# Head sums and segment sums with a 0/1 operand, as two one-pass products of the split other operand

## The chip, the cores and the metric

The kernel runs on one core of one Trainium2 chip, as one launch. The metric is device time in microseconds (us) of that launch; the median of three runs of the kernel before is 2382.67 us (2381.77 to 2384.16). The engines named below are PE (TensorE, matrix products), DVE (VectorE), ACT (ScalarE), POOL (GpSimd) and SP (SyncE, which issues the weight loads). Each engine works through its own queue in order; engines wait for one another by semaphores.

## The reference, cut to what matters

Two layers on 256 frames of width 2048, all in float32. Layer 0 has a parallel mixer (16 heads of RWKV-7 and 16 heads of Mamba-2 SSD, both of width 64), layer 1 chunked attention; each layer ends with a SwiGLU feed-forward. The change touches three sums of the mixer:

```
# RWKV-7: the norm of each head's key, and the bonus of each head
kk = heads(k * k_k)
kk = kk * lax.rsqrt(jnp.maximum(jnp.sum(kk * kk, axis=-1, keepdims=True), 1e-24))
...
bonus = jnp.sum(heads(r) * heads(k) * r_k, axis=-1, keepdims=True) * heads(v)
# SSD: decay between frames s and l of a chunk
A_cs = jnp.cumsum(Ac, axis=-1)
seg = A_cs[..., :, None] - A_cs[..., None, :]
L = jnp.where(causal, jnp.exp(jnp.where(causal, seg, 0.0)), 0.0)
```

The two sums run over the 64 channels of a head; seg[l, s] is the sum of A*dt over the frames after s up to l.

## The kernel before

All weights are streamed once from memory, in units of 256 rows by 512 columns (`stream`, lines 223 to 243). Each half of a unit is split into a high part in the one-pass float32r type (`hi`, a cast on ACT, line 240) and the remainder (`lo`, a subtraction on DVE, line 241). `mm_chunk` (lines 245 to 264) makes 512 output columns of all 256 frames: for each of 16 slices of the input, for each half of the frames, three products hi*hi, lo*hi, hi*lo (lines 260 to 262), so 96 products of 128x128 by 128x512 a chunk. The hi and lo tiles rotate through a few buffers, so the splits run only a few slices ahead of PE.

The mixer (`mixer0`, line 393) takes chunks 0 to 11 of the input projection `w_in`, called w_in#0 to w_in#11 here. Chunk 0 gives the low-rank inputs and dt; chunks 1 to 3 and 4 to 6 are the keys, receptances and values of the two halves of the RWKV heads (`rwkv_half`, line 481, called with hf = 0 and 1); 7 to 9 are the inputs of the SSD convolution (`conv_chunk`, line 771) and 10 and 11 its gate z (line 857). Then come the four chunks of the output projection `w_oab` and the rest of the network.

A half of RWKV goes through these steps. The squares kk of the keys (ACT, line 534) are summed over each head by a product with `blk`, a 128x128 matrix with ones where two channels share a head (ss, line 537), and turned into an inverse root by a logarithm and an exponential on ACT (lines 539, 540). DVE builds the tiles ar and bkv from it (lines 542 to 561). PE makes the blocks AA (line 576), DVE solves a triangular system by a row-by-row elimination in the tile NB (lines 590 to 595: 60 short instructions a half) and transposes the result three times into Sf and TG (lines 624, 625). The product ga (line 633) needs TG; from it runs a serial chain of small products over four chunks of 64 frames (gb, cx, cu, ch, cy; lines 637 to 719). The bonus is summed by a second product with `blk` (bo, line 603) and multiplied with the values on DVE (bv, line 604).

For SSD, POOL multiplies `gt` (ones where row > column) with the 8 heads' A*dt, which gives the tile L of 128 x 8 x 128 (line 826). Each head's slice is the stationary operand of a product with `tri` (ones where row <= column), four heads to a PSUM tile (sg, line 831); ACT takes the exponential (line 832), DVE multiplies it with the scores (line 833), and PE makes y (yd, line 838). There are two groups g and two halves t of the frames.

All products named so far in this part are float32 by float32, which the PE does in several passes: the trace shows two records for each.

The order on each queue is set by a list scheduler at build time, from priorities (streams of weights high) and its own table of costs; it also hands out buffers from pools. The pool `R` (tag r4) has nine buffers of 4 KB a partition: kk, ar, NB, TG, bv, bkt, uv, y and sq all live there.

```
kk[:, q, :] = square(k * k_k)                      # 534, ACT
pe.matmul(ps, lhsT=blk, rhs=kk[:, 2 * q2:2 * q2 + 2, :], start=True, stop=True)       # 537
act.activation(kk, kk, AF.Ln)                      # 539, after DVE's max with 1e-24
pe.matmul(ps[:, h, :], lhsT=L[:, 4 * h4 + h, :], rhs=tri, start=True, stop=True)      # 831
```

Of the kernel before, what the change touches and what calls it, by code (L numbers as in the profile page):

```python
# [13 lines left out]
ALU = mybir.AluOpType  # L14
# [128 lines left out]
def encoder_body(ctx: ExitStack, tc: tile.TileContext, A):  # L143
# [60 lines left out]
    def col(name, i=0, rows=P):  # L204
        return pf[:rows, _PF[name] + i:_PF[name] + i + 1]
# [187 lines left out]
    def mixer0(xt):  # L393
# [5 lines left out]
        with ExitStack() as mx:  # L399
# [5 lines left out]
            def r4(name, dt=F32, shape=(P, 4, T)):  # L405
                return R.tile(list(shape), dt, tag="r4", name=name)
# [71 lines left out]

            yst = []

            def rwkv_half(hf):
                f0 = 4 * hf
                w2 = R1.tile([96, 2, 512], F32, tag="wg", name=f"w2_{hf}")
# [6 lines left out]
                for which in range(3):  # L490
# [20 lines left out]
                    if which == 0:  # L511
# [20 lines left out]
                        kk = r4(f"kk{hf}")  # L532
                        for q in range(4):
                            act.activation(kk[:, q, :], k[:, q, :], AF.Square, scale=col("k_k", f0 + q))
                        for q2 in range(2):
                            ps = pra.tile([P, 2, T], F32, tag="ra", name=f"ss{hf}{q2}")
                            pe.matmul(ps, lhsT=blk, rhs=kk[:, 2 * q2:2 * q2 + 2, :], start=True, stop=True)
                            dve.tensor_scalar(kk[:, 2 * q2:2 * q2 + 2, :], ps, 1e-24, None, op0=ALU.max)
                        act.activation(kk, kk, AF.Ln)
                        act.activation(kk, kk, AF.Exp, scale=-0.5)  # L540
# [21 lines left out]
                    elif which == 1:  # L562
# [3 lines left out]
                        for q in range(4):  # L566
                            dve.scalar_tensor_tensor(r[:, q, :], r[:, q, :], col("r_k", f0 + q), a[:, q, :],
                                                     op0=ALU.mult, op1=ALU.mult)

                        AA = R1.tile([P, 32, 128], F32, tag="AA", name=f"AA{hf}")  # L570
                        for ch in range(4):
# [28 lines left out]
                bv = r4(f"bv{hf}")  # L600
                for q2 in range(2):
                    ps = pra.tile([P, 2, T], F32, tag="ra", name=f"bo{hf}{q2}")
                    pe.matmul(ps, lhsT=blk, rhs=r[:, 2 * q2:2 * q2 + 2, :], start=True, stop=True)
                    dve.tensor_tensor(c64(bv[:, 2 * q2:2 * q2 + 2, :]), c64(ps), bkv[:, 8 * q2:8 * q2 + 8, 128:192],
                                      op=ALU.mult)

# [189 lines left out]
            for g in range(2):  # L796
                for t in range(2):
# [2 lines left out]
            dve.tensor_tensor(SM.rearrange("p g t l -> p (g t) l"), ps.rearrange("p g t l -> p (g t) l"),  # L800
                              tri[:, None, :].broadcast_to([P, 4, 128]), op=ALU.mult)

            def hb(ap):
                return ap.rearrange("p (h v) -> p h v", v=64)

# [4 lines left out]
            for g in range(2):  # L810
# [12 lines left out]
                for t in range(2):  # L823
                    dve.tensor_tensor(hb(xc[:, t, :]), hb(xs[:, t, :]), hbc(dt[:, t, h8]), op=ALU.mult)
                    L = m4(f"L{g}{t}", (P, 8, 128))
                    pool.tensor_tensor(L, gt[:, None, :].broadcast_to([P, 8, 128]),
                                       adt[:, t, h8, None].broadcast_to([P, 8, 128]), op=ALU.mult)
                    for h4 in range(2):
                        ps = psa.tile([P, 4, 128], F32, tag="sa", name=f"sg{g}{t}{h4}")
                        for h in range(4):  # L830
                            pe.matmul(ps[:, h, :], lhsT=L[:, 4 * h4 + h, :], rhs=tri, start=True, stop=True)
                        act.activation(L[:, 4 * h4:4 * h4 + 4, :], ps, AF.Exp)
                    dve.tensor_tensor(L, L, SM[:, g, t, None, :].broadcast_to([P, 8, 128]), op=ALU.mult)
                    dve.tensor_tensor(hb(yg[:, t, :]), hb(xs[:, t, :]), hbc(rows[:, R_D + 8 * g:R_D + 8 * g + 8]),
                                      op=ALU.mult)
                    ps = psa.tile([P, 512], F32, tag="sa", name=f"yd{g}{t}")
                    for h in range(8):
                        pe.matmul(ps[:, 64 * h:64 * h + 64], lhsT=L[:, h, :], rhs=xc[:, t, 64 * h:64 * h + 64],
                                  start=True, stop=True)
                    dve.tensor_tensor(yg[:, t, :], yg[:, t, :], ps, op=ALU.add)  # L840
                    if t == 0:
                        xd = M.tile([P, 512], F32, tag="xd", name=f"xd{g}", bufs=1)
                        dve.tensor_tensor(hb(xd), hb(xc[:, 0, :]), hbc(dec[:, 0, h8]), op=ALU.mult)
                        ps = psa.tile([P, 512], F32, tag="sa", name=f"hs{g}")
                        pe.matmul(ps, lhsT=btm[:, g, :], rhs=xd, start=True, stop=True)
                        Hs = R2.tile([P, 512], F32, tag="H", name=f"Hs{g}")
                        act.copy(Hs, ps)
                    else:
                        ps = psa.tile([P, 512], F32, tag="sa", name=f"yo{g}")
                        pe.matmul(ps, lhsT=bc[:, 2 + g, P:T], rhs=Hs, start=True, stop=True)  # L850
                        yo = M.tile([P, 512], F32, tag="xd", name=f"yo{g}", bufs=1)
                        dve.tensor_tensor(hb(yo), hb(ps), hbc(dec[:, 1, h8]), op=ALU.mult)
                        dve.tensor_tensor(yg[:, t, :], yg[:, t, :], yo, op=ALU.add)
# [142 lines left out]
```

## Time and profile before

| what | value |
|---|---|
| median of three runs | 2382.67 us |
| the profiled execution's own time | 2384.66 us |
| its span in the trace | 2382.8 us (1.9 us less than its time) |
| mixer, up to the last transposes yb of the SSD output | about the first 451 us |
| PE busy in the span | 2352.1 us, 99% |
| DVE, ACT, POOL busy | 1428.8, 1267.5, 32.4 us |
| mean granted PE clock | 0.992 |

The busy time of PE is modelled from pipelined records: a product's record lasts longer than its share of the engine, so records overlap, and a busy share of 99% does not mean that no time is lost. Where a stage has waits, they are seen in the idle time before a group, in the distance between the starts of products, and in the granted clock (PEclk).

### The profile page before, as it was taken

The numbers are of one execution on the slowest core, as the hardware profiler recorded it, in microseconds if no ns is written. First come the engines' busy times: TensorE is split into PE (matmuls) and PEld (weight loads), VectorE is DVE, ScalarE is ACT, GpSimd is POOL, SyncE is SP. The second block draws the span as 40 slices with busy tenths as digits, with TensorE's granted clock in tenths as the row PEclk, the third lists the DMA queues.
The fourth block names the chain that finished last, engine by engine and source line by source line (L and its number), as shares of the span: only waits on it lengthen the run. The fifth ranks groups of instructions, "written<-read, shape, count | busy, mean of one in ns | idle before, by whom it ended". The sixth has DMA issues, their size and how long they took to land.

```text
span 2382.8 us, 31654 instructions
## 1 busy us (share of the span) xinstructions
PE 2352.1 (99%) x11426; PEld 1923.9 (81%) x11426; DVE 1428.8 (60%) x2380; ACT 1267.5 (53%) x2254; POOL 32.4 (1%) x61
## 2 busy tenths in 40 slices
PE   9999999999999999999999999999999999999998
PEld 7767777878888888888887888887888888888887
DVE  6876977765555555555557555557555555555554
ACT  6646545665545545544446555556555545454443
POOL 0000000000000000000000000000000000000000
PEclk9989999999999999999999999999999999999999
DMA  7434434666666666666665655565666666666664
GB/s 239 144 116 123 133 106 151 188 176 197 190 187 193 188 190 189 193 186 202 197 206 182 186 178 165 170 194 180 192 188 192 189 188 189 193 187 194 201 197 146
DMA packets 119357, 429.17 MB, mean 180 GB/s; under 512 B 13408, under 2 KB 13664, under 8 KB 119200
## 3 DMA queue, kind: packets, MB, share of 16 engines
q1 hardware_dynamic: 115280, 415.35, 57.2%
q0 software_dynamic: 2400, 9.18, 1.4%
q10 hardware_dynamic: 1520, 2.63, 0.4%
q8 instruction: 89, 1.46, 0.3%
q14 instruction: 68, 0.56, 0.1%
HBM read 425.01 MB, written 2.10 MB: 179 GB/s over the span
## 4 chain that ended last, share of the span: by engine, by line
PE 93%; DVE 4%; ACT 1%; DMA 1%; issue 1%; SPq 0%; DVEq 0%; ACTq 0%
PE mm_w_gu L260 13%; PE mm_w_gu L262 13%; PE mm_w_gu L261 13%; PE mm_w_dn L260 7%; PE mm_w_dn L262 7%; PE mm_w_dn L261 7%; PE mm_w_qkv L261 4%; PE mm_w_qkv L260 4%; PE mm_w_qkv L262 4%; PE mm_w_in L262 3%; PE mm_w_in L261 3%; PE mm_w_in L260 3%; PE mm_w_oab L260 1%; PE mm_w_oab L262 1%; PE mm_w_oc L262 1%; PE mm_w_oc L260 1%
## 5 line engine op out<-in xcount | busy, mean ns | idle before, releaser
L241 DVE TENSOR_TENSOR lo_w_gu<-raw_w_gu,hi_w_gu 128x512 fp32r<-128x512 f32 x704 | 485.8, 691 | 417.4 <-ACT hi_w_gu L240 414.9
L240 ACT CAST hi_w_gu<-raw_w_gu 128x512 fp32r<-128x512 f32 x704 | 438.4, 624 | 452.7 <-DVE lo_w_gu L241 404.9
L261 PE MATMUL mm_w_gu<-lo_w_gu,sh_f 128*128 128x512 f32 x1408 | 550.0, 391 | 0.0
L260 PE MATMUL mm_w_gu<-hi_w_gu,sh_f 128*128 128x512 f32 x1408 | 549.3, 390 | 0.6 <-ACT sh_f L299 0.5
L262 PE MATMUL mm_w_gu<-hi_w_gu,sl_f 128*128 128x512 f32 x1408 | 548.6, 390 | 0.0
L241 DVE TENSOR_TENSOR lo_w_dn<-raw_w_dn,hi_w_dn 128x512 fp32r<-128x512 f32 x352 | 242.8, 691 | 221.6 <-ACT hi_w_dn L240 221.0
L240 ACT CAST hi_w_dn<-raw_w_dn 128x512 fp32r<-128x512 f32 x352 | 219.0, 624 | 248.3 <-DVE lo_w_dn L241 238.6
L260 PEld LDWEIGHTS mm_w_gu<-hi_w_gu,sh_f 128*128 128x128 f32 x1408 | 264.3, 188 | 57.9 <-ACT sh_f L299 3.4
L262 PEld LDWEIGHTS mm_w_gu<-hi_w_gu,sl_f 128*128 128x128 f32 x1408 | 264.4, 188 | 55.5 <-DVE sl_f L300 1.2
L261 PEld LDWEIGHTS mm_w_gu<-lo_w_gu,sh_f 128*128 128x128 f32 x1408 | 264.4, 188 | 54.1 <-DVE lo_w_gu L241 0.3
L261 PE MATMUL mm_w_dn<-lo_w_dn,hh 128*128 128x512 f32 x704 | 274.1, 389 | 0.0
L262 PE MATMUL mm_w_dn<-hi_w_dn,hl 128*128 128x512 f32 x704 | 274.0, 389 | 0.0
L260 PE MATMUL mm_w_dn<-hi_w_dn,hh 128*128 128x512 f32 x704 | 273.9, 389 | 0.0
L241 DVE TENSOR_TENSOR lo_w_qkv<-raw_w_qkv,hi_w_qkv 128x512 fp32r<-128x512 f32 x192 | 132.2, 690 | 104.5 <-ACT hi_w_qkv L240 104.0
L240 ACT CAST hi_w_qkv<-raw_w_qkv 128x512 fp32r<-128x512 f32 x192 | 119.0, 621 | 110.3 <-DVE lo_w_qkv L241 64.8
L260 PE MATMUL mm_w_in<-hi_w_in,sh_in 128*128 128x512 f32 (+1 forms) x384 | 156.7, 408 | 1.7 <-ACT hi_w_in L240 1.7
L262 PE MATMUL mm_w_in<-hi_w_in,sl_in 128*128 128x512 f32 (+1 forms) x384 | 157.7, 411 | 0.0
L261 PE MATMUL mm_w_in<-lo_w_in,sh_in 128*128 128x512 f32 (+1 forms) x384 | 155.7, 405 | 0.0
L240 ACT CAST hi_w_in<-raw_w_in 128x512 fp32r<-128x512 f32 x184 | 112.3, 619 | 81.5 <-PE mm_w_in L262 71.5
L262 PEld LDWEIGHTS mm_w_dn<-hi_w_dn,hl 128*128 128x128 f32 x704 | 132.2, 188 | 27.6
L260 PEld LDWEIGHTS mm_w_dn<-hi_w_dn,hh 128*128 128x128 f32 x704 | 132.2, 188 | 27.3
L261 PEld LDWEIGHTS mm_w_dn<-lo_w_dn,hh 128*128 128x128 f32 x704 | 132.2, 188 | 27.2
(349 smaller groups left out, 2824.9 us busy)
## 6 DMA issues: line engine op xcount, KB each, us to landing
raw_w_gu<-in_w_gu SPq DMA_DIRECT2D x352, 512.0 KB, 3.6
raw_w_dn<-in_w_dn SPq DMA_DIRECT2D x176, 512.0 KB, 3.7
raw_w_qkv<-in_w_qkv SPq DMA_DIRECT2D x96, 512.0 KB, 3.6
raw_w_in<-in_w_in SPq DMA_DIRECT2D x92, 512.0 KB, 3.7
raw_w_oab<-in_w_oab SPq DMA_DIRECT2D x32, 512.0 KB, 4.2
raw_w_oc<-in_w_oc SPq DMA_DIRECT2D x32, 512.0 KB, 4.2
bias<-in_bias POOLq DMA_DIRECT2D x4, 768.0 KB, 6.6
x_in<-in_x SPq DMA_DIRECT2D x4, 512.0 KB, 9.0
```

The costliest lines, as they stand in the source:

```text
L240: act.copy(hi, raw[:, h, :])
L241: dve.tensor_tensor(lo, raw[:, h, :], hi.bitcast(F32), op=ALU.subtract)
L260: pe.matmul(o, lhsT=xh, rhs=h_[:, :width], start=k_ == 0, stop=False)
L261: pe.matmul(o, lhsT=xh, rhs=l_[:, :width], start=False, stop=False)
L262: pe.matmul(o, lhsT=xl, rhs=h_[:, :width], start=False, stop=k_ == nk - 1)
```

## The change

Each of the three products is replaced by two products whose 0/1 operand is stationary and is held in float32r (`blkr`, `gtr`, copied once by ACT), and whose moving operand is split into a high part (cast on ACT) and a remainder. `ones_mm` sums the two in PSUM. For the head sums the remainder is a subtraction on POOL of 128x512, two a tile (kl from kk, rl from r). For the segment sums A*dt itself is split once (adh, adl), POOL multiplies `tri` with both parts (Lr and Ll, twice the POOL products of before), and one product covers four heads, where four products stood.

```
@@ -478,6 +478,16 @@
 
             yst = []
 
+            blkr = R1.tile([P, P], F32R, tag="blkr", name="blkr")
+            act.copy(blkr, blk)
+            gtr = R1.tile([P, P], F32R, tag="gtr", name="gtr")
+            act.copy(gtr, gt)
+
+            def ones_mm(ps, ones, hi, lo):
+
+                pe.matmul(ps, lhsT=ones, rhs=hi, start=True, stop=False)
+                pe.matmul(ps, lhsT=ones, rhs=lo, start=False, stop=True)
+
             def rwkv_half(hf):
                 f0 = 4 * hf
                 w2 = R1.tile([96, 2, 512], F32, tag="wg", name=f"w2_{hf}")
@@ -532,9 +542,14 @@
                         kk = r4(f"kk{hf}")
                         for q in range(4):
                             act.activation(kk[:, q, :], k[:, q, :], AF.Square, scale=col("k_k", f0 + q))
+                        kh = r4(f"kh{hf}", F32R)
+                        kl = r4(f"kl{hf}", F32R)
                         for q2 in range(2):
+                            q4 = slice(2 * q2, 2 * q2 + 2)
+                            act.copy(kh[:, q4, :], kk[:, q4, :])
+                            pool.tensor_tensor(kl[:, q4, :], kk[:, q4, :], kh.bitcast(F32)[:, q4, :], op=ALU.subtract)
                             ps = pra.tile([P, 2, T], F32, tag="ra", name=f"ss{hf}{q2}")
-                            pe.matmul(ps, lhsT=blk, rhs=kk[:, 2 * q2:2 * q2 + 2, :], start=True, stop=True)
+                            ones_mm(ps, blkr, kh[:, q4, :], kl[:, q4, :])
                             dve.tensor_scalar(kk[:, 2 * q2:2 * q2 + 2, :], ps, 1e-24, None, op0=ALU.max)
                         act.activation(kk, kk, AF.Ln)
                         act.activation(kk, kk, AF.Exp, scale=-0.5)
@@ -566,6 +581,12 @@
                         for q in range(4):
                             dve.scalar_tensor_tensor(r[:, q, :], r[:, q, :], col("r_k", f0 + q), a[:, q, :],
                                                      op0=ALU.mult, op1=ALU.mult)
+                        rh = r4(f"rh{hf}", F32R)
+                        rl = r4(f"rl{hf}", F32R)
+                        for q2 in range(2):
+                            q4 = slice(2 * q2, 2 * q2 + 2)
+                            act.copy(rh[:, q4, :], r[:, q4, :])
+                            pool.tensor_tensor(rl[:, q4, :], r[:, q4, :], rh.bitcast(F32)[:, q4, :], op=ALU.subtract)
 
                         AA = R1.tile([P, 32, 128], F32, tag="AA", name=f"AA{hf}")
                         for ch in range(4):
@@ -600,7 +621,7 @@
                 bv = r4(f"bv{hf}")
                 for q2 in range(2):
                     ps = pra.tile([P, 2, T], F32, tag="ra", name=f"bo{hf}{q2}")
-                    pe.matmul(ps, lhsT=blk, rhs=r[:, 2 * q2:2 * q2 + 2, :], start=True, stop=True)
+                    ones_mm(ps, blkr, rh[:, 2 * q2:2 * q2 + 2, :], rl[:, 2 * q2:2 * q2 + 2, :])
                     dve.tensor_tensor(c64(bv[:, 2 * q2:2 * q2 + 2, :]), c64(ps), bkv[:, 8 * q2:8 * q2 + 8, 128:192],
                                       op=ALU.mult)
 
@@ -800,6 +821,11 @@
             dve.tensor_tensor(SM.rearrange("p g t l -> p (g t) l"), ps.rearrange("p g t l -> p (g t) l"),
                               tri[:, None, :].broadcast_to([P, 4, 128]), op=ALU.mult)
 
+            adh = M.tile([P, 2, 16], F32R, tag="adh", name="adh", bufs=1)
+            act.copy(adh, adt)
+            adl = M.tile([P, 2, 16], F32R, tag="adl", name="adl", bufs=1)
+            dve.tensor_tensor(adl, adt, adh.bitcast(F32), op=ALU.subtract)
+
             def hb(ap):
                 return ap.rearrange("p (h v) -> p h v", v=64)
 
@@ -823,12 +849,14 @@
                 for t in range(2):
                     dve.tensor_tensor(hb(xc[:, t, :]), hb(xs[:, t, :]), hbc(dt[:, t, h8]), op=ALU.mult)
                     L = m4(f"L{g}{t}", (P, 8, 128))
-                    pool.tensor_tensor(L, gt[:, None, :].broadcast_to([P, 8, 128]),
-                                       adt[:, t, h8, None].broadcast_to([P, 8, 128]), op=ALU.mult)
+                    Lr = r4(f"Lr{g}{t}", F32R, (P, 8, 128))
+                    Ll = r4(f"Ll{g}{t}", F32R, (P, 8, 128))
+                    for dst, ad in ((Lr, adh), (Ll, adl)):
+                        pool.tensor_tensor(dst, tri[:, None, :].broadcast_to([P, 8, 128]),
+                                           ad.bitcast(F32)[:, t, h8, None].broadcast_to([P, 8, 128]), op=ALU.mult)
                     for h4 in range(2):
                         ps = psa.tile([P, 4, 128], F32, tag="sa", name=f"sg{g}{t}{h4}")
-                        for h in range(4):
-                            pe.matmul(ps[:, h, :], lhsT=L[:, 4 * h4 + h, :], rhs=tri, start=True, stop=True)
+                        ones_mm(ps, gtr, Lr[:, 4 * h4:4 * h4 + 4, :], Ll[:, 4 * h4:4 * h4 + 4, :])
                         act.activation(L[:, 4 * h4:4 * h4 + 4, :], ps, AF.Exp)
                     dve.tensor_tensor(L, L, SM[:, g, t, None, :].broadcast_to([P, 8, 128]), op=ALU.mult)
                     dve.tensor_tensor(hb(yg[:, t, :]), hb(xs[:, t, :]), hbc(rows[:, R_D + 8 * g:R_D + 8 * g + 8]),
```

kh, kl, rh, rl, Lr and Ll are six new kinds of tile in the nine buffers of pool R. In the changed kernel's build the products Lr of group 0 get their buffers only behind the third chunk of the second half's serial chain, and the products sg and yd of group 0, which stood inside that chain, stand behind it.

The table of costs and the new tiles move instructions on all engines; the order of the weight loads on SP is the same. Three places follow.

First, ACT in half 0, between the squares kk and their logarithm (the second kk row behind the table load). hi_w_in are casts of streamed weights, lw, ar and c exponentials, kh the new casts. Before:

```order
L547 ACTIVATE wt_716<-c_691 128x16
L548 ACTIVATE lw_668<-lw_668 128x1024
L550 ACTIVATE ar_714<-c_691 128x8x64
L550 ACTIVATE ar_715<-c_691 128x8x64
L240 CAST hi_w_in_4_1_828<-raw_w_in_4_822 128x512
L539 ACT_TABLE_LOAD
L539 ACTIVATE kk_697<-kk_697 128x1024
L240 CAST hi_w_in_5_0_846<-raw_w_in_5_844 128x512
```

Now (one more kh and one more hi stand two rows higher):

```order
L549 CAST kh_706<-kk_701 128x512
L562 ACTIVATE wt_728<-c_695 128x16
L563 ACTIVATE lw_672<-lw_672 128x1024
L240 CAST hi_w_in_5_0_858<-raw_w_in_5_856 128x512
L565 ACTIVATE ar_726<-c_695 128x8x64
L240 CAST hi_w_in_5_1_862<-raw_w_in_5_856 128x512
L565 ACTIVATE ar_727<-c_695 128x8x64
L240 CAST hi_w_in_6_0_880<-raw_w_in_6_878 128x512
L566 ACTIVATE c_695<-c_695 128x1024
L240 CAST hi_w_in_6_1_884<-raw_w_in_6_878 128x512
L554 ACT_TABLE_LOAD
L554 ACTIVATE kk_701<-kk_701 128x1024
```

Ahead of the logarithm now stand two casts kh, four casts hi more, and the exponential c, which came behind it.

Second, DVE at the end of the second half's elimination (itmp and NB), where the transposes Sf and TG follow. lo_w_in are the remainders of streamed weights, xf, xc, xs and xd belong to SSD group 0. Before:

```order
L593 TENSOR_TENSOR itmp_2181<-NB_2179 64x58
L768 SCALAR_TENSOR_TENSOR xf_3076<-tr_cv_3271,hcv,xf_3076 128x253
L595 TENSOR_TENSOR NB_2179<-NB_2179,itmp_2181 64x2x29
L241 TENSOR_TENSOR lo_w_in_0_0_3659<-raw_w_in_0_3656,hi_w_in_0_0_3658 128x512
L593 TENSOR_TENSOR itmp_2181<-NB_2179 64x30
L595 TENSOR_TENSOR NB_2179<-NB_2179,itmp_2181 64x30
L624 STREAM_TRANSPOSE Sf_2513<-NB_2179 32x32x32
L241 TENSOR_TENSOR lo_w_in_0_1_3663<-raw_w_in_0_3656,hi_w_in_0_1_3662 128x512
L241 TENSOR_TENSOR lo_w_in_1_0_3681<-raw_w_in_1_3678,hi_w_in_1_0_3680 128x512
L624 STREAM_TRANSPOSE Sf_2513<-NB_2179 32x32x32
L241 TENSOR_TENSOR lo_w_in_1_1_3685<-raw_w_in_1_3678,hi_w_in_1_1_3684 128x512
L625 STREAM_TRANSPOSE TG_2180<-NB_2179 32x32x32
```

Now, some 30 rows ahead of TG:

```order
L241 TENSOR_TENSOR lo_w_in_0_1_3699<-raw_w_in_0_3692,hi_w_in_0_1_3698 128x512
L241 TENSOR_TENSOR lo_w_in_1_0_3717<-raw_w_in_1_3714,hi_w_in_1_0_3716 128x512
L614 TENSOR_TENSOR itmp_2215<-NB_2213 64x184
L850 TENSOR_TENSOR xc_3339<-xs_3326,dt 128x512
L616 TENSOR_TENSOR NB_2213<-NB_2213,itmp_2215 64x8x23
L862 TENSOR_TENSOR xs_3326<-xs_3326,rows 128x512
L241 TENSOR_TENSOR lo_w_in_1_1_3721<-raw_w_in_1_3714,hi_w_in_1_1_3720 128x512
L614 TENSOR_TENSOR itmp_2215<-NB_2213 64x168
L871 TENSOR_TENSOR xd_3366<-xc_3339,dec 128x512
L241 TENSOR_TENSOR lo_w_in_2_0_3739<-raw_w_in_2_3736,hi_w_in_2_0_3738 128x512
L616 TENSOR_TENSOR NB_2213<-NB_2213,itmp_2215 64x7x24
L850 TENSOR_TENSOR xc_3339<-xs_3326,dt 128x512
```

SSD's xf (the 128x1024 form), xc, xs and xd moved from behind TG to ahead of it, and nine remainders lo more than before stand ahead of TG (173 in the program, 164 before; for half 0's TG 88 and 85). On PE 55 products of the stream more stand ahead of the second ga (1023, before 968), 18 more ahead of the first (512, before 494), and 27 more ahead of the second half's first ss (660, before 633). Ahead of half 0's first key normalisation (line 542 before) DVE has 48 lo, before 44.

Third, PE at SSD group 1, behind the last products of w_in. sg are the segment sums, yd, hs and yo the products that use them. Before:

```order
L261 MATMUL mm_w_in_1_3872<-lo_w_in_5_1_3990,sh_in_126 128x512
L838 MATMUL yd_3606<-xc_3588,L_3590 128x64 x8
L845 MATMUL hs_3618<-xd_3616,btm 128x512
L262 MATMUL mm_w_in_1_3872<-hi_w_in_5_1_3989,sl_in_127 128x512
L260 MATMUL mm_w_in_0_3871<-hi_w_in_6_0_4007,sh_in_128 128x512
L261 MATMUL mm_w_in_0_3871<-lo_w_in_6_0_4008,sh_in_128 128x512
L262 MATMUL mm_w_in_0_3871<-hi_w_in_6_0_4007,sl_in_129 128x512
L831 MATMUL sg_3625<-cc,L_3623 128x128 x4
L831 MATMUL sg_3631<-cc,L_3623 128x128 x4
L260 MATMUL mm_w_in_1_3872<-hi_w_in_6_0_4007,sh_in_128 128x512
L261 MATMUL mm_w_in_1_3872<-lo_w_in_6_0_4008,sh_in_128 128x512
L262 MATMUL mm_w_in_1_3872<-hi_w_in_6_0_4007,sl_in_129 128x512
```

Now:

```order
L843 MATMUL xt_3620<-cc,xf_3403 128x128 x4
L488 MATMUL sg_3633<-Lr_3629,gtr 128x512
L489 MATMUL sg_3633<-Ll_3630,gtr 128x512
L488 MATMUL sg_3637<-Lr_3629,gtr 128x512
L489 MATMUL sg_3637<-Ll_3630,gtr 128x512
L866 MATMUL yd_3643<-xc_3626,L_3628 128x64 x8
L873 MATMUL hs_3655<-xd_3653,btm 128x512
L488 MATMUL sg_3665<-Lr_3661,gtr 128x512
L489 MATMUL sg_3665<-Ll_3662,gtr 128x512
L488 MATMUL sg_3669<-Lr_3661,gtr 128x512
L489 MATMUL sg_3669<-Ll_3662,gtr 128x512
L866 MATMUL yd_3675<-xc_3626,L_3660 128x64 x8
```

Between xt and the second yd of group 1 stood 44 products of the stream; now there is none, and the 20 products between the transposes tr_cv of chunk 9 and xt are the last of w_in.

## Rows read from the trace of the kernel before

**Rows 1.** The page: busy time of the engines.

```profile
PE 2352.1 (99%) x11426; PEld 1923.9 (81%) x11426; DVE 1428.8 (60%) x2380; ACT 1267.5 (53%) x2254; POOL 32.4 (1%) x61
```

**Rows 2.** Busy time by stage; columns: us, PE, PEld, DVE, ACT, POOL, PEclk, DMA, GB/s.

```profile
62.00:80.00 18.00, 18.00 (x76) 13.71 (x75) 11.40 (x19) 17.61 (x33) 0.54 (x1) 1.00 0.47 139
80.00:156.50 76.50, 70.87 (x366) 55.61 (x364) 72.32 (x145) 39.66 (x70) 3.07 (x6) 1.00 0.48 143
156.50:193.00 36.50, 36.45 (x481) 25.42 (x483) 14.05 (x28) 10.99 (x22) 0.94 (x4) 0.81 0.25 74
233.50:328.00 94.50, 87.06 (x442) 69.05 (x444) 91.34 (x182) 54.18 (x94) 5.20 (x7) 1.00 0.48 144
328.00:365.20 37.20, 37.06 (x547) 29.50 (x547) 21.09 (x35) 13.17 (x26) 2.51 (x3) 0.91 0.16 53
365.20:431.00 65.80, 62.52 (x301) 51.06 (x300) 50.76 (x83) 41.93 (x73) 3.79 (x2) 0.95 0.52 161
```

**Rows 3.** Waits of PE, 60 to 450 us: total, times, longest.

```profile
PE ga L633 <- DVE TG L625: 6.4, 2, 3.9
PE yd L838 <- DVE L L833: 3.3, 1, 3.3
```

**Rows 4.** Timeline of PE: start, duration; at ss, then at sg.

```profile
69.45 0.39 PE L262 MATMUL mm_w_in<-hi_w_in,sl_in 128*128 128x512 f32 x1
69.68 1.06 PE L537 MATMUL ss<-kk,cc 128*128 128x512 f32 x2
70.18 0.80 PE L260 MATMUL mm_w_in<-hi_w_in,sh_in 128*128 128x512 f32 x1
70.81 0.40 PE L261 MATMUL mm_w_in<-lo_w_in,sh_in 128*128 128x512 f32 x1
...
413.30 1.95 PE L831 MATMUL sg<-cc,L 128*128 128x128 f32 x16
415.00 0.49 PE L260 MATMUL mm_w_in<-hi_w_in,sh_in 128*128 128x512 f32 x1
```

**Rows 5.** Timeline of ACT behind the second table of half 0.

```profile
78.69 1.06 ACT L540 ACTIVATE kk<-kk 128x1024 f32<-128x1024 f32 x1
79.65 1.13 ACT L240 CAST hi_w_in<-raw_w_in 128x512 fp32r<-128x512 f32 x2
80.69 1.06 ACT L551 ACTIVATE c<-c 128x1024 f32<-128x1024 f32 x1
```

**Rows 6.** Timeline of POOL at two of its four products.

```profile
316.45 2.14 POOL L826 TENSOR_TENSOR L<-cc,adt 128x1024 f32<-128x1024 f32 x1
...
334.15 1.90 POOL L826 TENSOR_TENSOR L<-cc,adt 128x1024 f32<-128x1024 f32 x1 [15.56 <-PE xt L817]
```

**Rows 7.** Timeline of DVE in the same stretches.

```profile
315.38 0.23 DVE L593 TENSOR_TENSOR itmp<-NB 64x84 f32<-64x84 f32 x1
...
316.75 1.91 DVE L593 TENSOR_TENSOR itmp<-NB 64x58 f32<-64x58 f32 x1
...
332.95 0.69 DVE L824 TENSOR_TENSOR xc<-xs,dt 128x512 f32<-128x512 f32 x1
...
334.67 1.92 DVE L824 TENSOR_TENSOR xc<-xs,dt 128x512 f32<-128x512 f32 x1 [1.03 <-ACT xs L818]
```

**Rows 8.** Groups by line and form, 0 to 452 us: count | busy, mean ns.

```profile
L241 DVE TENSOR_TENSOR lo_w_in<-raw_w_in,hi_w_in 128x512 fp32r<-128x512 f32 x184 | 124.7, 687 | 35.1 <-ACT hi_w_in L240 34.3
L833 DVE TENSOR_TENSOR L<-L,SM 128x1024 f32<-128x1024 f32 x4 | 4.9, 1225 | 3.5 <-ACT L L832 3.5
L768 DVE SCALAR_TENSOR_TENSOR xf<-tr_cv,hcv,xf 128x254 f32<-128x254 f32 x8 | 3.7, 472 | 0.0
L779 DVE SCALAR_TENSOR_TENSOR xf<-tm,xf 128x1024 f32<-128x1024 f32 x2 | 2.4, 1214 | 1.7 <-ACT tm L778 1.7
L818 ACT COPY xs<-xt 128x512 f32<-128x512 f32 x4 | 2.2, 586 | 1.4 <-PE xt L817 1.4
L778 ACT ACTIVATE tm<-xf 128x1024 f32<-128x1024 f32 x2 | 2.1, 1062 | 1.7 <-DVE xf L768 1.7
```

## The prediction

> **What bounds the kernel now.** I read the page's engine line first: PE is busy 99% of the span, the other engines 60% and less [rows 1]. So outside the mixer the kernel is as fast as PE's products, and the change touches nothing there. It can act in the first 450 us only, where I read next the busy time by stage. The reader is to see two things in it [rows 2]. From 62 to 80 us ACT is full (17.61 of 18.00 us), and where the two halves eliminate DVE is (72.32 of 76.50, 91.34 of 94.50): there the product stream has cover enough, and what is put on ACT or DVE delays the next tile. And in the serial chains (156.5 to 193, 328 to 365.2) PE's granted clock falls, to 0.81 and 0.91 on average. Full speed is 2.4 GHz, the lower level 1.2, so the lost time is 0.19 x 36.5 = 6.9 us in half 0 and 0.09 x 37.2 = 3.3 us in half 1; the second chain has more to do (547 products against 481 in about the same time), because SSD group 0 stands in it. From 365 to 431 us it is 0.95: 0.05 x 65.8 = 3.3 us. Last I read the waits of PE: 6.4 us at the two ga, for TG, and 3.3 at a yd [rows 3].
>
> **The change part by part.** *PE's own work.* Two neighbouring stream products start 0.23 us apart (69.45, 69.68). From 69.45 to 70.81 stand two of them and one ss, so the ss costs 1.36 - 0.46 = 0.90 us; its two new products cost 0.46. That saves 0.45 us for each of four ss and four bo, 3.6 us. The 16 records of sg take 1.70 us (413.30 to 415.00) for two tiles, 0.85 each; a pair costs 0.46, so eight tiles save 3.1 us. Together -6.7 us [rows 4].
>
> *What costs nothing.* blkr, gtr, adh and adl are four small operations ahead of a need for them: at most one 128x512 cast each (0.57 us, 1.13 for two [rows 5]), so 0 to 2.3 us; I take 0, since they stand where ACT and DVE wait for the weights. The casts rh lie beside the elimination, where ACT has 39.66 of 76.50 us to do [rows 2]; without that cover they would cost 4 x 0.57 = 2.3 us.
>
> *POOL.* Its product of 128x1024 takes 2.14 and 1.90 us [rows 6]. In both cases the DVE instruction beside it with two tiles as inputs became long: 1.91 us for 64x58, where a larger one took 0.23, and 1.92 us for xc, where the other took 0.69 [rows 7]. So POOL's product and such a DVE instruction don't run side by side, and a new POOL product costs DVE its own length. The Trainium skill has this as a rule (SBUF — State Buffer, "SBUF: two separate sides"): the pair of ports that GpSimd shares with VectorE is an exclusive lock, held for a whole instruction, between a GpSimd operation that reads SBUF and a VectorE operation with two SBUF inputs. The trace agrees (1.91 for 0.23 us); by the rule the price below stands, without it case B holds. A subtraction of 128x512 has no row on POOL; half the length gives 0.95, the whole 1.90. I take 0.95, as elements scale, so 1.9 us a half for rl.
>
> *Half 0.* Ahead of the first logarithm ACT gets two kh and four hi more (6 x 0.57 = 3.4 us) and c (1.06 [rows 5]): 4.5 us. ACT is full there, so DVE's first key normalisation comes 4.5 us later; in the time it does four lo that stood later (48 against 44 ahead of it; 4 x 0.69 = 2.7 [rows 8]), so it is 1.8 us behind its own work. Then come rl, 1.9. In all three lo more stand ahead of TG (88 against 85 in the two orders; 2.1). TG comes 1.8 + 1.9 + 2.1 = 5.8 us later. PE reaches ga 18 x 0.23 - 4 x 0.45 = 2.3 us later, so the wait there grows by 3.5. If DVE weren't late at the normalisation and POOL cost it nothing, it would shrink by 0.2; with 1.90 us a subtraction it grows by 5.4.
>
> *Half 1.* PE has 27 stream products more ahead of ss1 (660 against 633), 6.2 us less 1.8 for what is saved; with the wait of half 0 that is 7.9 us later. DVE has 3.5 more ahead (nearly all lo), so it is 4.4 late. rl adds 1.9, and a POOL product L that stood beside this elimination [rows 6] goes, -1.9: 0. Ahead of TG stand nine lo more (6.2) and xf, two xc, two xs, one xd (1.21 + 5 x 0.69 = 4.7 [rows 8]): 10.9. TG comes 15.3 later. PE reaches ga by 55 x 0.23 = 12.7, plus 0.9 for the eight transposes xt, which now stand ahead, less 3.6: 10.0 later, and the 3.5 of half 0 on top. The wait grows by 1.8 more. Both waits: +5.3 us (bounds -0.7, where DVE keeps up, and +10, with POOL at the long price and xf waiting for its transposes).
>
> *The second chain.* sg, yd, hs of group 0 go behind it. With the filling of half 0 it should look like half 0's: 6.9 instead of 3.3 us lost to the clock, +3.6 (0 if the clock stays at 0.91).
>
> *The tail.* Group 0 and group 1 now stand close together, with little stream left. Behind yo of group 0 DVE has three additions (2.1), twelve taps xf (12 x 0.47 = 5.6), three lo (2.1), then the last xf (1.21) behind ACT's tm (1.06): 12.1 us to the xt of chunk 9 [rows 8]. PE has 20 products and the transposes, about 6.7, so it waits 5.4. From xt to the first yd of group 1: PE 0.44, the copy xs 0.59, xc 0.69, xs 0.69, xd 0.69, xc 0.69, L 1.22 make 5.0 [rows 8] beside 1.8 of PE's work: 3.2. From there to the second yd: xs 0.69, four lo 2.8, L 1.22 make 4.7 beside 0.4 + 0.9, so 3.4, about 4 with the exponentials. Group 0's own two yd and the first yb I put at 3 together, and the lower clock after such waits at 2, as after the 3.3 us wait of before. That makes 17.6, where before had 3.3 of waiting and 3.3 of clock [rows 2, 3]: +11.0 (bounds 0, if the waits overlap to no more than those of before, and +18, if PE does seven us of work more at the lower clock).
>
> Sum: 5.3 + 3.6 + 11.0 - 6.7 = +13.2. The profiled execution took 2384.66 us (span 2382.8 and 1.9 around it), 2.0 above the median of 2382.67. On the median: 2395.9.
>
> **The rivals.** *B, POOL works beside DVE.* Then rl costs nothing: 1.9 us less in half 0, and in half 1, where rl and the product L cancel, nothing. That gives 2394. Against it stand the two lengthened rows [rows 7]; for it, that they are only two.
> *C, not slower.* The lists were remade so that DVE has work in what was its waiting for ACT from 62 to 80 us; if ACT hands the logarithm over no later than DVE ends its four lo (lateness at the first key normalisation 0 or below), TG keeps pace with PE, the ga waits stay at 6.4, and the tail's waits, fed by remainders done earlier, stay within 6.6. Then the saved products show: 2382.67 - 6.7 = 2376. It decides at 1.8 us of lateness; ACT's 17.61 of 18.00 us speaks against it [rows 2].
> *D, the tail as before.* +5.3 + 3.6 - 6.7 = +2.2: 2385. For it speaks that one DVE queue stands behind all these waits, so that a long first one shortens the next; against it, that no stream product stands between xt and the second yd.
> *E, the long prices.* POOL at 1.90 a subtraction and the lower clock on through the tail: +10 + 3.6 + 18 - 6.7 = +24.9, so 2407.6.
> That the sums don't get shorter on PE I give no chance of its own: both forms stand in the rows.
>
> **How the numbers follow.** The forecast has 0.48, with 2388 to 2403 as its own range; B 0.12; C 0.10; D 0.16; E 0.14. Less than about 0.2% (4.8 us, 2377.9 to 2387.4) can't be told from no change in this kernel. Faster: most of C, 0.08. Within: the rest of C and two thirds of D, 0.12. Slower: 0.80. The range from 2382 to 2409 leaves out C and the upper end of E.
>
> **What would show it.** In the changed kernel's profile: pairs of ss, bo and sg 0.46 us long on PE; POOL's eight subtractions at about 0.95 us, with DVE instructions of two inputs lengthened beside them; PE's wait for TG up from 6.4 to about 11.7 us; the mean clock in the second chain down to about 0.81; waits of PE for xf at xt (5), and for L at the yd of group 1 (3 and 4). Wrong it would be if TG waits stay near 6.4 and those of the tail near 3.3, or if the chain keeps 0.91.

## The result, and the profile after

The changed kernel takes 2406.69 us (median of five runs, 2404.64 to 2407.52) against 2383.56 for the kernel before in the same session: ratio 1.0096, 95% interval 1.0083 to 1.0109, slower by 23 us. The first product of the SwiGLU weights starts at 536.53 us, before at 513.71. So the whole 22.8 us are lost ahead of it, in the mixer and the output projection behind it.

Waits of PE in the profile after (total, times, longest), to be read against [rows 3]:

```profile
PE yd L866 <- DVE L L861: 11.7, 3, 5.7
PE xt L843 <- DVE xf L800: 5.6, 1, 5.6
PE ga L654 <- DVE TG L646: 5.3, 2, 2.7
PE ss L489 <- POOL kl L550: 1.8, 2, 1.5
```

The wait for TG has not grown (6.4 before). The waits for L and xf, which stand behind the second chain, have: 17.3 us where there were 3.3.

Busy time by stage, after: the second chain, then the stretch behind it (columns as in [rows 2]); below, the kernel before in that stretch:

```profile
340.00:376.00 36.00, 35.28 (x430) 24.91 (x430) 14.22 (x28) 11.77 (x24) 7.09 (x6) 0.86 0.25 75
376.00:444.00 68.00, 50.68 (x206) 38.99 (x205) 45.50 (x60) 28.27 (x48) 10.90 (x5) 0.77 0.25 83
```

```profile
376.00:444.00 68.00, 64.62 (x314) 53.07 (x312) 50.44 (x84) 44.38 (x80) 3.79 (x2) 0.95 0.57 178
```

In the same 68 us PE ran 206 records instead of 314, at a granted clock of 0.77 instead of 0.95. POOL is busy three times as long, DVE and ACT less: no engine is full there, each waits for another.

PE at two bo, after (start, duration), against [rows 4]:

```profile
120.51 0.39 PE L488 MATMUL bo<-rh,blkr 128*128 128x512 f32 x1
120.74 0.39 PE L489 MATMUL bo<-rl,blkr 128*128 128x512 f32 x1
120.97 0.40 PE L260 MATMUL mm_w_in<-hi_w_in,sh_in 128*128 128x512 f32 x1
```

A pair takes 0.46 us, as forecast: the change does what it says, and PE's own work is some 6.8 us less (an estimate from these spacings). The pairs of ss don't stand so close: there PE waits for kl, 1.8 us in all.

POOL's new products by form (count | busy, mean ns):

```profile
L855 POOL TENSOR_TENSOR Lr<-cc,adh 128x1024 fp32r<-128x1024 f32 x4 | 9.1, 2266 | 3.5 <-PE cu L695 3.3 <-PE sg L488 0.2
L855 POOL TENSOR_TENSOR Ll<-cc,adl 128x1024 fp32r<-128x1024 f32 x4 | 8.5, 2121 | 3.2 <-PE ch L704 3.2
L550 POOL TENSOR_TENSOR kl<-kk,kh 128x512 fp32r<-128x512 f32 x4 | 6.6, 1675 | 9.3 <-issue 5.1 <-ACT kh L549 4.2
L589 POOL TENSOR_TENSOR rl<-r,rh 128x512 fp32r<-128x512 f32 x4 | 5.9, 1507 | 56.5 <-ACT rh L588 56.5
```

A subtraction takes 1.5 to 1.7 us on average, not the 0.95 that I scaled from [rows 6]. The shortest took 1.28 us, one of them at 231.00 with DVE idle or reading PSUM; up to 2.08 us are reached beside DVE's lo. POOL and then DVE ahead of group 0's first yd, after:

```profile
377.03 2.39 POOL L855 TENSOR_TENSOR Lr<-cc,adh 128x1024 fp32r<-128x1024 f32 x1
379.38 2.34 POOL L855 TENSOR_TENSOR Ll<-cc,adl 128x1024 fp32r<-128x1024 f32 x1
381.90 2.88 POOL L855 TENSOR_TENSOR Lr<-cc,adh 128x1024 fp32r<-128x1024 f32 x1 [0.17 <-PE sg L488]
```

```profile
376.98 2.98 DVE L241 TENSOR_TENSOR lo_w_in<-raw_w_in,hi_w_in 128x512 fp32r<-128x512 f32 x2
379.89 1.86 DVE L745 TENSOR_SCALAR mean<-mean 128x16 f32<-128x16 f32 x1
...
382.93 4.69 DVE L241 TENSOR_TENSOR lo_w_in<-raw_w_in,hi_w_in 128x512 fp32r<-128x512 f32 x2
...
389.35 1.21 DVE L861 TENSOR_TENSOR L<-L,SM 128x1024 f32<-128x1024 f32 x1
```

Two lo take 1.3 us elsewhere ([rows 8]: 0.69 each), here 2.98 and 4.69. The L that the yd waits for comes behind them, at 389.35.

### The profile page after: what moved, and what is told of

Same layout as the page of the kernel before. It is cut to its first block, busy times and chain, and to the rows that moved or that the text cites. A ratio compares the mean times of both kernels' runs of the same rounds, so it can differ in the third digit from the quotient of the medians.

```text
span 2405.7 us, 31601 instructions
## 1 busy us (share of the span) xinstructions
PE 2360.1 (98%) x11378; PEld 1927.2 (80%) x11378; DVE 1436.8 (60%) x2381; ACT 1270.1 (53%) x2263; POOL 54.5 (2%) x73
## 4 chain that ended last, share of the span: by engine, by line
PE 92%; DVE 5%; issue 1%; ACT 1%; DMA 0%; POOL 0%; DVEq 0%; SPq 0%; ACTq 0%
PE mm_w_gu L260 13%; PE mm_w_gu L261 13%; PE mm_w_gu L262 13%; PE mm_w_dn L261 7%; PE mm_w_dn L262 7%; PE mm_w_dn L260 7%; PE mm_w_qkv L260 4%; PE mm_w_qkv L262 4%; PE mm_w_qkv L261 4%; PE mm_w_in L262 2%; PE mm_w_in L261 2%; PE mm_w_in L260 2%; DVE lo_w_in L241 2%; PE mm_w_oab L260 1%; PE mm_w_oab L262 1%; PE mm_w_oab L261 1%
## 5 line engine op out<-in xcount | busy, mean ns | idle before, releaser
L241 DVE TENSOR_TENSOR lo_w_in<-raw_w_in,hi_w_in 128x512 fp32r<-128x512 f32 x184 | 132.1, 728 | 37.2 <-ACT hi_w_in L240 36.5
```

Of the source, the lines that this page charges most:

```text
L241: dve.tensor_tensor(lo, raw[:, h, :], hi.bitcast(F32), op=ALU.subtract)
```

## The experiments

One table first, to which the runs refer. Each ratio is to runs of the kernel before in the same session; the median of that kernel was 2382.1 to 2384.4 us in the sessions, so kernels of different sessions are best compared by their ratios. TG is the start of half 1's TG on DVE, w_gu that of the first SwiGLU product (us, from each timeline).

| kernel | ratio (95%) | TG | w_gu | between |
|---|---|---|---|---|
| before | 1 | 325.96 | 513.71 | 187.8 |
| after | 1.0096 (1.0083 to 1.0109) | 337.04 | 536.53 | 199.5 |
| head_only | 1.0069 (1.0056 to 1.0083) | 344.02 | 530.65 | 186.6 |
| seg_only | 1.0039 (1.0026 to 1.0052) | 325.90 | 522.72 | 196.8 |
| hold_group0 | 1.0001 (0.9992 to 1.0009) | 323.56 | 511.55 | 188.0 |
| pool_m | 1.0111 (1.0097 to 1.0125) | 344.87 | 539.95 | 195.1 |
| bo_only | 1.0045 (1.0033 to 1.0058) | 330.71 | 522.37 | 191.7 |
| ss_only | 1.0065 (1.0052 to 1.0078) | 337.80 | 528.57 | 190.8 |
| stock_head | 1.0052 (1.0040 to 1.0065) | 340.57 | 523.78 | 183.2 |
| fill_tail | 1.0091 (1.0075 to 1.0106) | 336.63 | 534.13 | 197.5 |
| bo_behind_tg | 0.9990 (0.9982 to 0.9999) | 328.80 | 510.42 | 181.6 |
| head_behind_tg | 1.0031 (1.0019 to 1.0043) | 334.40 | 520.55 | 186.2 |
| seg_late_pool | 1.0012 (1.0003 to 1.0021) | 325.47 | 515.14 | 189.7 |
| both_holds | 1.0048 (1.0036 to 1.0060) | 330.31 | 522.43 | 192.1 |

**The parts apart.** head_only has the diff's hunks on kk, r and bo alone, seg_only those on adt, Lr and Ll alone.

> Only the head sums (ss, bo) are changed; the segment sums are those of before. Theory 1 (the loss comes from the SSD groups that stand close together behind the second chain, because Lr and Ll wait for buffers of pool R; the head sums are nearly even): 2379 to 2388 us, since 3.6 us of products go, TG keeps about its 6 us of waits, and group 1, which here too stands without stream products between its steps, costs a few us. Rival (the casts and POOL subtractions of the head sums, which delay the inverse root by 4.7 and 6.8 us, carry the loss): 2395 us or more.

> Only the segment sums are changed; the head sums are those of before. Theory 1: most of the loss is here, 2394 to 2404 us, with a wait at the first yd and a low clock behind the second chain; somewhat less than the whole, as 52 products instead of 20 stand ahead of the xt of chunk 9. Rival (head sums carry the loss): 2378 to 2386 us.

Measured 2401.2 and 2393.6 us: both lose, 17 and 9 us, and the two together are somewhat more than the whole (26 for 23). Theory 1, with its even head sums, fell; seg_only is just below its range. In the table the head sums move TG and leave the time behind it, and the segment sums leave TG and lengthen the time behind it. A later TG isn't lost time as such: PE makes stream products meanwhile, and in the changed kernel it lost nothing up to the second ga (-0.8 us, in the account further on).

**The place alone, and the buffers.** hold_group0 edits the kernel before, pool_m the changed one:

```
+ with tc.issue_after(hold[0].ins):   # POOL's last memset of H in half 1
      pool.tensor_tensor(L, ...)
```

```
- Lr = r4(...); Ll = r4(...)
+ Lr = M.tile([P, 8, 128], F32R, tag="m4", ...); Ll = M.tile(..., tag="m4", ...)
```

> The kernel before, with the POOL products L held back until POOL's last memset H of the second chain: no instruction is added, only the place of SSD group 0 moves behind the chain, as in the changed kernel. Theory 1 (the place costs, not the new work): 2389 to 2400 us, the second chain losing about as much to the clock as the first, and waits at the yd. Rival (the eight long POOL products Lr and Ll, beside which DVE stands still, cost it): 2382 to 2386 us, as POOL has only its four products here.

> The changed kernel with Lr and Ll in the four buffers of pool M in place of R: group 0's sg and yd stand ahead of and inside the second chain, the operations are the same. Theory 1: 2384 to 2396 us (group 0 no longer crowds, but group 1's steps still stand without stream products between them). Rival (the new POOL work costs wherever it stands, some 17 us in all beside DVE): 2400 us or more.

Measured 2383.71 (no change) and 2410.96 us. The place of group 0 behind the chain costs nothing by itself, and moving it back to the front gains nothing (the intervals of pool_m and after overlap): in pool_m its DVE work stands ahead of TG, which starts 18.9 us later than before, and PE waits 7.6 us at sg for Lr and Ll, so place and POOL work aren't parted there.

**Which head sum.** bo_only and ss_only are head_only without the edits on kk, and without those on r and bo.

> Only the bonus sums bo are changed (casts rh, POOL subtractions rl, two one-pass products). Theory 2 (the first one, that Lr and Ll push group 0 behind the chain and the place costs, has fallen: group 0 held there alone cost nothing): a mixer with a fixed stock of 1152 w_in products loses time where they run out. What delays DVE's inverse root or TG makes the order spend them earlier, and group 1's steps then stand bare, with waits and a low clock. Behind group 1's xt are left 56 products in the kernel before, 26 with group 0 held, 16 with the segment sums, none with the head sums or all. Here 32 are left and the inverse root isn't touched: 2381 to 2387 us, no change. Rival (rl on POOL and rh on ACT, beside a full DVE, are what costs in the head sums): 2390 to 2400 us.

> Only the sums ss of the squared keys are changed (kh, kl, two one-pass products). Theory 2: 16 products are left behind group 1's xt and the inverse root comes 4 to 7 us later, so most of the loss of the head sums is here, 2390 to 2399 us. Rival (rl and rh cost): 2381 to 2387 us.

Measured 2393.74 and 2399.71 us: ss_only nearly as theory 2 said (0.7 us above its range), bo_only not, though its inverse root comes 1.5 us earlier than before. The stock of products left is no measure by itself: 32 are left in bo_only, 26 in hold_group0, which lost nothing. What bo_only shares with the others is a later TG (4.8 us): SSD group 0's last xf, xc, xs and xd stand ahead of it on DVE.

**The low clock, and the stock.** fill_tail is the changed kernel with this, called with 20, 20, 8 and 14 ahead of group 0's first yd, group 1's xt and its two yd; stock_head is head_only with the end of the last w_in chunk held.

```
+ def fill(ps, n):
+     for _ in range(n):
+         pe.matmul(ps, lhsT=gtr, rhs=st[0][0][:, 0:2, :], start=True, stop=True)
```

```
+ with tc.issue_after(keep.ins) if keep is not None and kt >= KEEP else ExitStack():   # KEEP = 7; keep: last xt of group 1
      for k_, h_, l_ in held: ...
```

> The changed kernel with 62 more products of 128x512 (14 us), whose results are overwritten, in PE's queue ahead of the first yd of group 0 (20), the xt of chunk 9 (20) and the two yd of group 1 (8 and 14), where PE waits for DVE. If the low clock behind the second chain is a cost of its own, 11.3 us there against 2.7 before, and follows from PE standing idle, it goes for the most part: 2396 to 2402 us, although PE has 14 us more to do. If the slow products only run in time that PE would have waited anyway: 2404 to 2412 us.

> Only the head sums changed, and the last 54 products of w_in (slices 7 to 15 of its last chunk) held in PE's queue until behind group 1's xt, where the kernel before has 56. Theory 2: the waits and the low clock at group 1's yd go, 2386 to 2394 us against 2401. Rival (the tail is bound by DVE's and ACT's chain, so the wait only moves ahead, to xt): 2398 to 2404 us.

fill_tail took 2404.98 us, in the rival's range. The filled stretch:

```profile
376.00:444.00 68.00, 58.46 (x270) 45.42 (x269) 47.78 (x64) 29.71 (x50) 10.37 (x5) 0.94 0.26 86
```

The clock came up from 0.77 to 0.94 with 14 us of work added, and the time stayed the same: 1.0091 for 1.0096, well within the intervals. So the slow products ran for the most part in time that PE would have waited anyway, or the filling took what the clock gave back; the run doesn't split the two. stock_head took 2395.68 us, between the two expectations: some 4 us better than head_only by the ratios, 5.5 by the medians, but 6.4 us of waiting now stand at the xt of chunk 9. So with the stock kept, PE waits there for DVE all the same.

**The two causes taken away.** bo_behind_tg and head_behind_tg have the first edit, seg_late_pool the second, both_holds both:

```
+ with tc.issue_after(tgs[1].ins) if n == 8 else ExitStack():   # half 1's TG
      dve.scalar_tensor_tensor(dst, th, 1.0, dst, op0=ALU.add, op1=ALU.mult)
```

```
+ with tc.issue_after(lexp[-1].ins) if lexp else ExitStack():   # group 0's last Exp of L
+     adh, adl = adsplit(g)
```

> As bo_only, with one edge more: the last xf of SSD group 0 (and so xt, xc, xs, xd, sg, yd) stands behind half 1's TG in DVE's queue, as in the kernel before. Theory 3 (the stock of products left has fallen as a measure: bo_only left 32 and lost 11.7 us. From the second TG to the end of the mixer the time is nearly the same in before, bo_only, ss_only and head_only, 184.6 to 189.7 us, so what counts is when that TG comes, and the head sums let SSD group 0's DVE work pass ahead of it): TG ends at 328 us instead of 332.7, and 2381 to 2387 us. Rival (the passed work only has to be done later instead, before the end): 2391 to 2396 us.

> As head_only, with the same edge: SSD group 0's DVE work behind half 1's TG. Theory 3: TG ends at 337 to 340 us instead of 346.0 (the later inverse root, 8.7 us at half 1, stays), and 2391 to 2396 us against 2401. Rival (no gain): 2399 to 2403 us.

> As seg_only, with the split of A*dt done apart for each group and group 1's held behind group 0's last exponential in ACT's queue, so that group 1's four POOL products of 1.9 us and more no longer run ahead of group 0's first yd, where they held up DVE. Theory (the loss of the segment sums is POOL's doubled work, beside which DVE instructions with two tiles stand still: with the same place and half the POOL products, hold_group0 lost nothing): the 5.7 us wait at group 0's first yd falls below 2, and 2384 to 2389 us against 2393.6. Rival (the products Lr and Ll come late, whether DVE is held up or not): 2391 to 2396 us.

> The changed kernel with both: SSD group 0's DVE work behind half 1's TG, and group 1's POOL products behind group 0's last exponential. If the two causes add: 2391 to 2399 us against 2406.7. If either only moves the wait: 2401 us or more.

All four came out on the side of theory 3 and of the theory on POOL: 2379.97, 2389.88, 2385.90 and 2393.50 us, the first two by 1 us better than their range. So holding SSD group 0's DVE work behind TG is a cure, whole for bo_only and in part for head_only. That it works by an earlier TG is not shown for the bonus sums. In head_behind_tg TG comes 9.6 us earlier than in head_only, and w_gu 10.1. But in bo_behind_tg TG comes only 1.9 us earlier than in bo_only (2.8 later than before, where I expected the same), and w_gu 12.0. The other 10.1 us lie behind TG. bo_only there, then bo_behind_tg (columns as in [rows 2]):

```profile
340.00:376.00 36.00, 36.00 (x450) 26.77 (x449) 13.41 (x26) 11.77 (x23) 0.61 (x2) 0.87 0.15 45
376.00:444.00 68.00, 62.80 (x295) 50.35 (x293) 52.67 (x87) 42.79 (x78) 4.35 (x2) 0.92 0.48 156
```

```profile
340.00:376.00 36.00, 34.91 (x411) 27.98 (x412) 20.51 (x36) 14.73 (x27) 0.61 (x2) 1.00 0.13 35
376.00:444.00 68.00, 66.74 (x336) 54.51 (x335) 55.94 (x98) 47.12 (x88) 3.80 (x2) 1.00 0.60 190
```

The clock is full where it was 0.87 and 0.92 (10.1 us lost, worked out as in the prediction), and PE's waits for L at yd fall from 4.5 to 0.7 us. The hold also leaves 50 products behind group 1's xt, for 32. So for bo theory 3 came out on the right side without its reason, and whether the clock, the waits or the products left are the cause there stays open. bo_behind_tg is below the kernel before (0.9990, interval below 1), by 2.4 us; its four sums save 1.8 us, and its clock behind the chain is 1.00 for 0.95, so the gain is not all shown to be the saved products. The L that group 0's first yd waits for, on DVE in seg_only, and in seg_late_pool:

```profile
376.78 1.21 DVE L847 TENSOR_TENSOR L<-L,SM 128x1024 f32<-128x1024 f32 x1
```

```profile
370.61 1.23 DVE L855 TENSOR_TENSOR L<-L,SM 128x1024 f32<-128x1024 f32 x1 [0.32 <-ACT L L854]
```

It comes 6.2 us earlier, with TG only 0.4 earlier, and PE's wait of 5.7 us is gone; but for the split of A*dt by groups, nothing changed except when POOL makes group 1's products. PE's waits for L, in the same two kernels:

```profile
PE yd L852 <- DVE L L847: 9.8, 2, 5.7
```

```profile
PE yd L860 <- DVE L L855: 4.2, 1, 4.2
```

The wait that is left, at a yd of group 1, is little more than the 3.3 us of before; where the 3.5 us lie that seg_late_pool still loses is not shown.

With both edits some 12 of the 23 us come back; 11 are left against the kernel before in that session. What is left of the head sums (7.5 us in head_behind_tg) is as large as the delay of its inverse root: DVE's first key normalisation of half 1, before, after, and in head_behind_tg:

```profile
233.48 0.88 DVE L542 SCALAR_TENSOR_TENSOR kk<-k,pf,kk 128x256 f32<-128x256 f32 x2 [1.60 <-ACT kk L540]
```

```profile
240.23 0.88 DVE L557 SCALAR_TENSOR_TENSOR kk<-k,pf,kk 128x256 f32<-128x256 f32 x2 [1.60 <-ACT kk L555]
```

```profile
241.34 0.88 DVE L556 SCALAR_TENSOR_TENSOR kk<-k,pf,kk 128x256 f32<-128x256 f32 x2 [1.60 <-ACT kk L554]
```

That this delay is what costs them was not tried by itself: no run put the casts kh ahead of the others. The last 4 us or so of both_holds are about what seg_late_pool still loses, and stay open too.

## Why the prediction was right, and where it was not

The side and the range were right: slower, 2406.7 within 2382 to 2409. The size was not: 13.2 us forecast on the median, 23.1 measured, outside the likeliest case's own range (2388 to 2403). That the wide range held it is in part luck, since a term too dear by 6 us stood against one too cheap by 14. By the start of each product less the work ahead of it, the 22.8 us are -6.8 of work, -0.8 up to the second ga, +5.5 in the second chain and +24.9 behind it; forecast were -6.7, +5.3, +3.6 and +11.0.

*PE's own work* held. *What costs nothing* shows up in none of PE's waits; it was not tried by itself.

*Half 0 and half 1* were too dear by 6.1 us. The inverse root came 4.7 us later (4.5 forecast), in half 1 6.75 (7.9). But TG of half 1 came 11.1 us later, not 15.3, and of half 0 3.7, not 5.8. The price of rl failed. DVE beside it, after, while POOL subtracts from 104.02 to 106.98:

```profile
104.00 0.68 DVE L601 TENSOR_TENSOR AA<-aa,cc 128x512 f32<-128x512 f32 x1
104.60 1.25 DVE L241 TENSOR_TENSOR lo_w_in<-raw_w_in,hi_w_in 128x512 fp32r<-128x512 f32 x1
105.77 1.27 DVE L601 TENSOR_TENSOR AA<-aa,cc 128x512 f32<-128x512 f32 x2
```

Three of the four instructions there are AA, which read a PSUM tile and one SBUF tile, and they keep their 0.68 us; only the lo loses 0.6. I charged POOL's whole length, 1.9 us. The old product L, whose going I had set against rl in half 1, had held its instruction up by 1.7 us (1.91 for 0.23, [rows 7]), so there the two don't cancel. And the rows above start 0.60 us apart though each is 0.68 long: a DVE instruction of 128x512 behind another costs 0.60, where I charged its length of 0.69. kl, for which I had charged nothing, cost PE 1.8 us at ss. So the wait for TG fell by 1.1 where I had it grow by 5.3, and the sign that I had named for it, 11.7 us, did not come (5.3).

*The second chain* was right in kind and too small: 3.6 forecast for 5.5 us. The clock there was 0.86 over 36 us, 5.0 us lost where I had expected 6.9 like half 0's; that is 1.7 more than the 3.3 of before. A wait at cx takes 0.7. The rest lies in longer distances between the chain's small products, which the profile doesn't list as waits; I can't split it further.

*The tail* is the term that was mis-sized, 11.0 for 24.9 us. Its waits for xt (5.6 measured, 5.4 forecast), the first yd of group 1 (2.0 for 3.2) and the second (4.0 for 4) came as worked out. Two entries were wrong. Group 0's yd and the first yb stood at 3 together, while its first yd alone waited 5.7: I had priced POOL's products on the elimination only, and not in the stretch where all eight now stand, the last four of them ahead of DVE's work for that yd. And I put 2 us on the low clock after such waits: it was low (1.2 GHz) for 34 of the 65 us from 382 to 447, and products slowed by it took about 11 us more there, 2.7 before (each product's distance to the next less its usual one, counted up to once the usual one). How much of those would come back with a full clock is what fill_tail left unsplit.

*The rivals.* B fell: POOL's products do hold up DVE. D fell with the tail. E came nearest (2407.6), but by luck: its 10 us for the waits on TG were -0.8, its 18 for the tail 24.9, and a subtraction cost the elimination even less than at my price. C's point of decision, the lateness at the first key normalisation, was rightly read in that it came late (4.7 us) and the kernel got slower; bo_behind_tg, which has next to no lateness there (80.06 us for 79.78), is the one that gained.

On causes the forecast was half right. It had "Group 0 and group 1 now stand close together, with little stream left" for the whole tail; hold_group0 shows that close together costs nothing while POOL has two products ahead of group 0's yd instead of eight. The head sums lose in good part because SSD's DVE work stands ahead of TG, as the two holds show. From TG to w_gu it takes 182 to 192 us in every kernel with the old segment sums, however much of the stream was done before; but this spread of 10 us is the whole of what bo_behind_tg gains behind TG, so the time of TG alone doesn't settle the end. The part of the later inverse root is argued, not shown.

## What to carry to other kernels

Work saved on the engine that is 99% busy gained nothing here, in a stage whose end is set by a chain through other engines. Find what that chain hands over (here TG) and list every instruction that the new order lets pass ahead of it; then hold these back in a run of their own, because the lateness of the handover alone is a poor price (1.9 us earlier, 12.0 gained). Work given to an idle POOL is not free: look at what DVE does beside each POOL product, instruction by instruction, and move POOL's products to where DVE reads PSUM or isn't waited for. Measure the parts apart before the whole; here one of them gained a little, once the order was held.

## What was not expected of the hardware

One DVE instruction with a single SBUF input stood still beside POOL as well: the scaling of mean, 128x16, took 1.86 us at 379.89, 0.16 in the kernel before and 0.17 in seg_late_pool, where POOL's products come later. The reduction that makes mean, one SBUF input too, kept its 1.22 us beside a POOL product (375.85). The scaling before:

```profile
367.74 0.16 DVE L724 TENSOR_SCALAR mean<-mean 128x16 f32<-128x16 f32 x1
```

The Trainium skill (SBUF — State Buffer, "SBUF: two separate sides") names two kinds of VectorE operation that take the shared ports, those in a 2-port mode and those with two SBUF inputs. With its single input the scaling isn't of the second kind; whether it ran in a 2-port mode no run here shows. POOL's own products become longer too where DVE is busy: 1.90 us alone, 2.34 to 2.88 us from 377 to 387. It goes much further where DVE works on two SBUF tiles without a gap. In pool_m one Lr takes 7.92 us: it starts while DVE runs lo, itmp, NB, xs, xd, xc and L back to back, up to 330.7, and ends only behind DVE's next gap of 1.09 us (POOL, then DVE):

```profile
324.55 7.92 POOL L855 TENSOR_TENSOR Lr<-cc,adh 128x1024 fp32r<-128x1024 f32 x1 [0.94 <-PE sg L489]
```

```profile
331.80 0.69 DVE L868 TENSOR_TENSOR xs<-xs,yd 128x512 f32<-128x512 f32 x1 [1.09 <-PE yd L866]
```

And a subtraction of two tiles of 128x512 takes at least 1.28 us, though a product of 128x1024 with broadcast inputs takes 1.90: the time doesn't scale with the elements alone.
